# A planned order of instructions: modulation dot products move from GpSimd to VectorE, one chunk of them to the FFN, and the planner's durations change

## The chip, the cores and the metric

The kernel runs on one core of a Trainium2 chip. The metric is device time in microseconds from one launch, the median of several runs. The engines are named as in the profile: PE is TensorE, with PEld its weight loads; DVE is VectorE, ACT ScalarE, POOL GpSimd, SP the engine that issues most DMAs.

## The reference, cut to what matters

Two layers run over 512 latent tokens with a context of 256 tokens. Layer 0 mixes tokens by bidirectional gated linear attention (GLA, 4 heads), layer 1 by latent attention (MLA, 8 heads), and each is followed by a gated ConvFFN. Every sub-layer is modulated: six vectors of 1024 numbers per layer (shift, scale and gate of the mixer, then of the FFN) come from a condition, one condition for the latent tokens and one for the context.

```python
def ada_modulation(cond, w, b):
    m = jax.nn.silu(cond) @ w + b
    return jnp.split(m, 6, axis=-1)

def modulate(x, g, shift, scale):
    return rmsnorm(x, g) * (1 + scale[..., None, :]) + shift[..., None, :]

x = x + g1[:, None, :] * o
x = x + g2[:, None, :] * conv_ffn(modulate(x, norm_ffn[i], sh2, sc2), ...)
```

The six vectors are called chunks 0 to 5 here. Chunks 0 and 1 feed the first norm, 2 is the gate of the mixer (`g1`), 3 and 4 are shift and scale of the FFN's norm, and 5 is the gate of the FFN (`g2`), which is first needed where the FFN's first down product is added to the residual.

## The kernel before, in words

All activations are kept feature-major, [128 features, 768 tokens] per tile, and each weight tile of [128, 1024] is loaded into a ring of three staging buffers (`ws`), split exactly into a high part on ACT (`wh`) and a low part on DVE (`wl`), and used in three products on PE (`mm3`).

**The modulations.** A chunk has 8 tiles of 128 features. `ada` loads one tile of weights (`wa`, in the same ring of three as `ws`) and forms one dot product per condition against the condition's row `cb`. A dot on DVE is one instruction with an accumulated sum (`junk` in the rows), followed by a short read of the accumulator. The other way, in `ada_dot`, is a product on POOL (`wa<-wa,cb`, over the weights in place) and then a sum on ACT (`wa<-wa` with an accumulator); the staging buffer is free only after the ACT instruction. With two conditions, the first goes to DVE and the second to POOL and ACT. In layer 1, chunks 2 to 5 are needed for one condition only, and the two ways alternate (`flip`).

**Where they are made.** Chunks 0 and 1 of layer 0 are made in the start. In `gla`, each of the four heads is emitted by `weave`, which interleaves three streams: the products of this and the next head, the chain of the attention itself (`core`: transposes `ktp`, scores `scp` and `A`, states `stp` and `R`, outputs `ops` and `o`, transposed outputs `Got`), and one chunk of modulations (2, 4, 3, 5 in this order). In the FFN of layer 0, `extra(i)`, called behind the i-th pair of feature tiles, makes the modulations of layer 1, three tiles a time from i = 2.

**What sets the order.** `Later` records every instruction and `flush` puts them in the order of a list schedule: each engine takes the first recorded of those whose operands and buffers are ready, with durations from `cost` and delays from `after`. Only the order comes from there. On the chip, each engine executes its list in order and waits at the head of it, SP's DMA issues too. All instructions are issued from one line of `flush`, so that they share one line number (L263) in the profile.

Of the kernel before, what the change touches and what calls it, by code (L numbers as in the profile page):

```python
# [13 lines left out]
ALU = mybir.AluOpType  # L14
# [16 lines left out]
# columns of the vector table  # L31
# [14 lines left out]
# columns of the table of constants  # L46
# [6 lines left out]
# how the start is divided: feature tiles whose first modulations are products of the tensor engine, and  # L53
# (tile, shift or scale, condition) of those whose products GpSimd makes
# [5 lines left out]
MOD_STAGE = (0, 1, 2)  # tiles whose modulation weights come in the buffers of the other weights  # L60
# what arrives in turn: modulation weights of a feature tile, two tiles of the first weights, the context
START_LOADS = ("m0", "m1", "w0", "w1", "w2", "m3", "m2", "m5", "m4", "ctx", "w3", "m7", "m6")
COND_AFTER = (3, 7)  # tiles of squares after which the two conditions are taken
CTX_NORM = 5  # the step of the first products at which the norm of the context comes
CTX_LAG = 5  # steps of the context behind those of the latent tokens, not before its norm
NORM_POOL = (3, 6)  # the feature tiles of a latent norm that GpSimd and ScalarE modulate


def weave(*streams):
    """Emits the steps of several streams in proportion: (generator, its expected total, where it starts).  # L70
    A step is its time on the tensor engine, or its share of the total."""
    live = [[g, total, sum(start)] for g, total, *start in streams]
    while live:
        s = min(live, key=lambda x: x[2])
        try:
            step = next(s[0])
            s[2] += step[0] if isinstance(step, tuple) else step / s[1]
        except StopIteration:
            live.remove(s)


def paced(units):
    """Steps of units of work that count as equally long: (generator, its expected total)."""
# [18 lines left out]
class Later:  # L102
    """Records instructions and emits them when a pool ends, in the order of a list schedule.

    Every engine takes the first recorded of the instructions whose operands and buffers are ready; the costs are
    those of the guide. Only the order comes from here: Tile finds all waits anew, in the instructions so ordered."""
# [3 lines left out]
    def __init__(self, tc):  # L110
        self.tc, self.real = tc, tc.nc
        self.ops, self.preload = [], None
        self.seen = {}  # tile -> its accesses in this batch
        self.done = {}  # tile -> when its accesses end, from earlier batches
        self.held, self.tags = {}, {}  # tag, and tile of it -> (tag, the tiles in its buffers)
        self.old = {}  # tile -> the one before in its buffer
        self.free = dict.fromkeys(self.ENGINES, 0.6) | {"sync": 2.2}
        self.table = None
        # from the end of an instruction on one engine to the start of one that needs it on another
# [21 lines left out]
    def record(self, engine, op, args, kw):  # L141
        if op == "preload_act_table_set":
            # goes before the next activation, if that changes the table
# [5 lines left out]
        for x, write in aps:  # L149
            row = math.prod(x.tensor.shape[1:])  # L150
            lo = hi = x.offset % row
            # the elements of a partition: from lo to hi, and if they are few, which
# [19 lines left out]
        self.ops.append((engine, op, args, kw, preload, deps, {x.name for x, _ in aps}, *self.cost(engine, op, args, kw, aps)))  # L172

    @staticmethod
    def cost(engine, op, args, kw, aps):
        """time on the engine, and the activation table"""
# [4 lines left out]
        if engine == "tensor":  # L181
            if op == "transpose":
                return max(0.107, x.shape[-1] / 2400.0), None
            full = (args[1] if len(args) > 1 else kw["lhsT"]).dtype == F32
            return (max(0.213, n / 600.0) if full else max(0.107, n / 2400.0)), None
# [5 lines left out]
        n = max(math.prod(y.shape[1:]) for y, _ in aps)  # L191
        if engine == "vector":
# [3 lines left out]
        return (0.16 * n if kw.get("op") == ALU.pow else 0.1 + n / 450.0), None  # L196
# [1460 lines left out]
```

## Time and profile before

| what | value |
| --- | --- |
| median of 3 runs | 1679.93 us (1679.58 to 1681.09) |
| profiled execution, span from first to last instruction | 1679.1 us |
| PE busy in it | 1611.4 us (96%) |
| DVE busy | 1116.0 us (66%) |
| ACT busy | 720.4 us (43%) |
| POOL busy | 298.9 us (18%) |
| mean granted TensorE clock | 0.989 |

The profile gives no time of its own for the profiled execution beside its span; the median of the runs is 0.8 us above the span. The stages follow each other: the start (to about 80 us), the four GLA heads (80 to 385), the output product and the norm of the FFN (385 to 460), the FFN of layer 0 (460 to 1000), MLA (1000 to 1330) and the FFN of layer 1. A busy share near 100% on PE means that matmuls follow each other closely; PE's time at half clock counts as busy, so the granted clock (PEclk) has to be read beside it.

### The profile page before, as it was taken

What the parts mean: (1) busy time and instruction counts of PE and PEld (TensorE: products, weight loads), DVE (VectorE), ACT (ScalarE), POOL (GpSimd) and SP (SyncE); (2) the same over time, 40 slices, a digit from 0 to 9 for tenths busy, and PEclk for the clock granted to TensorE, in tenths of its full rate; (3) what the DMA queues carried; (4) which work ended last, traced back from release to release, by engine and by line L of the source; (5) the groups of instructions that cost most, each with busy time, mean ns of one, the idle gap of its engine ahead of it and who ended that gap; (6) DMA issues with size and microseconds to landing.
All of it is one profiled execution on the core that took longest, in us unless ns stands there. A gap on an engine that the chain in (4) does not pass through costs nothing.

```text
span 1679.1 us, 22918 instructions
## 1 busy us (share of the span) xinstructions
PE 1611.4 (96%) x9086; PEld 1386.0 (83%) x9086; DVE 1116.0 (66%) x1773; ACT 720.4 (43%) x1253; POOL 298.9 (18%) x170
## 2 busy tenths in 40 slices
PE   7899889889999999999999999999999999999999
PEld 4688778778888888888888888788889888888887
DVE  7977777885677855655544567777776765555554
ACT  4555444552443533323322336666653533333331
POOL 3223233330112411111100020334400100000000
PEclk9999999999999999999999999999999999999999
DMA  8222223233133343333331222100031232232232
GB/s 320 99 93 96 93 86 111 76 116 142 38 113 121 131 151 126 126 126 126 126 101 64 76 109 79 40 15 26 20 120 47 69 113 98 90 101 99 90 100 76
DMA packets 50079, 165.59 MB, mean 99 GB/s; under 512 B 5554, under 2 KB 7346, under 8 KB 49972
## 3 DMA queue, kind: packets, MB, share of 16 engines
q1 hardware_dynamic: 49332, 162.04, 28.2%
q0 software_dynamic: 640, 2.10, 0.3%
q8 instruction: 71, 1.16, 0.3%
q14 instruction: 36, 0.29, 0.1%
HBM read 159.92 MB, written 4.19 MB: 98 GB/s over the span
## 4 chain that ended last, share of the span: by engine, by line
PE 78%; DVE 10%; issue 5%; ACT 3%; DMA 2%; POOL 1%; SPq 0%; POOLq 0%; DVEq 0%; ACTq 0%
PE G L263 59%; PE Gs L263 4%; PE av L263 2%; PE ukv L263 2%; DVE K L263 2%; PE Gu L263 2%; DVE junk L263 2%; PE uq L263 1%; DMA wa<-in_wada 1%; PE pt L263 1%; DVE hl L263 1%; PE ops L263 1%; PE vps L263 1%; DVE R L263 1%; PE stp L263 1%
## 5 line engine op out<-in xcount | busy, mean ns | idle before, releaser
L263 PE MATMUL G<-hh,wh 128*128 128x512 f32 (+1 forms) x1416 | 507.0, 358 | 1.2 <-DVE x L263 1.2
L263 PE MATMUL G<-hl,wh 128*128 128x512 f32 (+2 forms) x1416 | 494.1, 350 | 0.2 <-DVE hl L263 0.2
L263 PE MATMUL G<-hh,wl 128*128 128x512 f32 (+1 forms) x1400 | 491.9, 351 | 0.0
L263 DVE TENSOR_TENSOR wl<-ws,wh 128x1024 fp32r<-128x1024 f32 (+3 forms) x178 | 222.4, 1251 | 270.2 <-ACT wh L263 268.7
L263 ACT CAST wh<-ws 128x1024 fp32r<-128x1024 f32 (+3 forms) x186 | 189.5, 1020 | 441.9 <-PE G L263 422.8
L263 PEld LDWEIGHTS G<-hh,wh 128*128 128x128 f32 x1416 | 267.4, 189 | 36.3 <-DVE x L263 1.4
L263 PEld LDWEIGHTS G<-hl,wh 128*128 128x128 f32 (+1 forms) x1416 | 266.7, 188 | 36.9 <-DVE hl L263 0.7
L263 PEld LDWEIGHTS G<-hh,wl 128*128 128x128 f32 x1400 | 264.3, 189 | 34.5
L263 POOL TENSOR_TENSOR wa<-wa,cb 128x1024 f32<-128x1024 f32 x64 | 168.4, 2634 | 524.3 <-DVE mod L263 263.2
L263 PE MATMUL G<-ph,wh 128*128 128x512 f32 (+1 forms) x512 | 181.8, 355 | 2.3 <-DVE z L263 2.3
L263 PE MATMUL G<-ph,wl 128*128 128x512 f32 (+1 forms) x512 | 182.1, 356 | 0.0
L263 PE MATMUL G<-pl,wh 128*128 128x512 f32 (+1 forms) x512 | 181.7, 355 | 0.0
L263 DVE SCALAR_TENSOR_TENSOR z<-G,vec,z 128x511 f32<-128x511 f32 x248 | 151.0, 651 | 1.7 <-ACT z L263 0.9
L263 DVE CUSTOM_DVE_ANT_0 junk<-wa,cb 128x1024 bf16<-128x1024 f32 x75 | 109.9, 1465 | 49.2 <-DMA wa<-in_wada 49.0
L263 PEld LDWEIGHTS G<-ph,wh 128*128 128x128 f32 x512 | 96.2, 188 | 16.9 <-issue 2.6
L263 PEld LDWEIGHTS G<-pl,wh 128*128 128x128 f32 x512 | 96.1, 188 | 14.8
L263 PEld LDWEIGHTS G<-ph,wl 128*128 128x128 f32 x512 | 96.1, 188 | 13.9
L263 ACT ACTIVATE wa<-wa 128x1024 f32<-128x1024 f32 x64 | 67.6, 1057 | 66.4 <-POOL wa L263 66.3
L263 DVE SCALAR_TENSOR_TENSOR x<-G,mod,x 128x512 f32<-128x512 f32 (+1 forms) x112 | 64.8, 610 | 35.2 <-PE G L263 34.7
L263 ACT ACTIVATE z<-G,vec 128x768 f32<-128x768 f32 (+1 forms) x82 | 72.4, 883 | 3.1 <-PE G L263 2.3
L263 ACT ACTIVATE z<-z 128x768 f32<-128x768 f32 (+1 forms) x44 | 32.5, 739 | 93.2 <-DVE z L263 93.2
L263 DVE SCALAR_TENSOR_TENSOR y<-G,mod,y 128x512 f32<-128x512 f32 (+1 forms) x72 | 49.2, 688 | 21.3 <-PE G L263 20.7
(343 smaller groups left out, 2673.0 us busy)
## 6 DMA issues: line engine op xcount, KB each, us to landing
wa<-in_wada SPq DMA_DIRECT2D x90, 512.0 KB, 3.5
ws<-in_wup SPq DMA_DIRECT2D x88, 512.0 KB, 3.3
ws<-in_wdn SPq DMA_DIRECT2D x44, 512.0 KB, 3.5
ws<-in_win SPq DMA_DIRECT2D x13, 512.0 KB, 3.3
ws<-in_wmd SPq DMA_DIRECT2D x9, 512.0 KB, 3.3
ws<-in_wv SPq DMA_DIRECT2D x8, 512.0 KB, 3.7
ws<-in_wog SPq DMA_DIRECT2D x8, 512.0 KB, 3.6
ws<-in_womh SPq DMA_DIRECT2D x8, 512.0 KB, 5.6
```

Of the source, the lines that this page charges most:

```text
L263: getattr(getattr(self.real, engine), op)(*args, **kw)
```

## The change

1. `ada_chunk`, which makes the chunks of layer 0 after the start, calls `ada` with `alone=True`: both dots of a tile are DVE instructions, without POOL and ACT. The modulations of layer 1 stay as they were.
2. Chunk 5 leaves the GLA heads. Chunks 2, 4 and 3 are spread over the four heads (6, 7, 6 and 5 tiles, where there were 8 in each). Chunk 5 is made by `extra(0)` and `extra(1)`, four tiles each, in the FFN of layer 0.
3. `cost` has other durations for transposes, products, scans and powers, and a new function `shares` marks instructions of DVE and POOL that, in the plan, can't run beside each other: the plan starts one after the other's end.

```diff
+        self.port = {"vector": 0.0, "gpsimd": 0.0}
...
             if op == "transpose":
-                return max(0.107, x.shape[-1] / 2400.0), None
+                return 0.109, None
-            return (max(0.213, n / 600.0) if full else max(0.107, n / 2400.0)), None
+            return (max(0.22, n / 590.0) if full else max(0.109, 0.0063 + n / 2296.0)), None
...
+        if op == "tensor_tensor_scan":
+            return 0.07 + n / 480.0, None
...
-        return (0.16 * n if kw.get("op") == ALU.pow else 0.1 + n / 450.0), None
+        return (0.9 + 0.17 * n if kw.get("op") == ALU.pow else 0.1 + n / 450.0), None
+
+    @staticmethod
+    def shares(engine, op, aps):
+        reads = [x for x, write in aps if not write and x.space != PSUM and math.prod(x.shape[1:]) > 1]
+        if engine == "gpsimd":
+            return bool(reads) and op != "dma_start"
+        fast = op in ("tensor_scalar", "tensor_copy") and aps[0][0].space != PSUM
+        return engine == "vector" and (len(reads) > 1 or bool(reads) and fast)
...
-            cost, table = ops[i][7:]
+            cost, table, shares = ops[i][7:]
+            if shares:
+                t = max(t, self.port[e])
...
             self.free[e] = end[i] = t + cost
+            if shares:
+                self.port["gpsimd" if e == "vector" else "vector"] = t + cost
...
-    def ada(self, layer, chunk, nt, conds):
+    def ada(self, layer, chunk, nt, conds, alone=False):
         wa = self.ada_load(layer, chunk, nt)
         self.flip ^= len(conds) == 1
         for c in conds:
-            self.ada_dot(wa, layer, chunk, nt, c, None if self.flip or len(conds) == 2 and c == 0 else wa)
+            self.ada_dot(wa, layer, chunk, nt, c, None if alone or self.flip or (len(conds) == 2 and c == 0) else wa)
...
-    def ada_chunk(self, layer, ch, conds=(0, 1)):
-        for nt in range(8):
-            self.ada(layer, ch, nt, conds)
+    def ada_chunk(self, layer, ch, conds=(0, 1), nts=range(8)):
+        for nt in nts:
+            self.ada(layer, ch, nt, conds, True)
             yield 1.0
+        if nts[-1] < 7:
+            return
         self.ada_bias(layer, ch, conds)
...
-                (self.ada_chunk(0, 2), 8.0),
+                (self.ada_chunk(0, 2, nts=range(6)), 6.0),
...
-                (self.ada_chunk(0, 4), 8.0),
+                (seq(self.ada_chunk(0, 2, nts=range(6, 8)), self.ada_chunk(0, 4, nts=range(5))), 7.0),
...
-                (self.ada_chunk(0, 3), 8.0),
+                (seq(self.ada_chunk(0, 4, nts=range(5, 8)), self.ada_chunk(0, 3, nts=range(3))), 6.0),
...
-                (self.ada_chunk(0, 5), 8.0),
+                (self.ada_chunk(0, 3, nts=range(3, 8)), 5.0),
...
             def extra(i):
+                if i < 2:
+                    run_all(self.ada_chunk(0, 5, nts=range(4 * i, 4 * i + 4)))
```

What the plan makes of it is seen in the engines' lists. First POOL from the end of the start through the four heads, before: `wa` are the products of modulations, `orr` the inverse root of the output norm of a head, `nr` that of a norm of tokens, `ny` a norm's product.

```order
L263 TENSOR_TENSOR wa<-wa,cb 128x1024 x6
L263 TENSOR_TENSOR orr<-orr,mhalf 128x6
L263 TENSOR_TENSOR wa<-wa,cb 128x1024 x8
...
L263 TENSOR_TENSOR wa<-wa,cb 128x1024 x2
L263 TENSOR_TENSOR nr<-nr,mhalf 128x4
```

And now, up to the FFN of layer 0:

```order
L280 TENSOR_TENSOR prod<-wa_117,cb 128x1024
L280 TENSOR_TENSOR nr<-nr,mhalf 128x2
L280 TENSOR_TENSOR orr<-orr,mhalf 128x6 x4
L280 TENSOR_TENSOR nr<-nr,mhalf 128x4
L280 TENSOR_TENSOR ny<-x_3197,nrb 128x512
L280 TENSOR_TENSOR ny<-x_3200,nrb 128x512
L280 TENSOR_TENSOR nr<-nr,mhalf 128x2
L280 TENSOR_TENSOR wa<-wa,cb 128x1024 x32
```

The 32 products between the start and the output product are gone; the four `orr` stand alone, and the 32 products for layer 1 remain behind the norm of the FFN.

Second, DVE in the first head, in the forward states (`R` with its factor `cf` carries the state from one block to the next, `A` are masked scores, `junk` is a dot, `ISA mod` its accumulator). Before:

```order
L263 TENSOR_TENSOR R_703<-stp,R_700 128x256
L263 TENSOR_TENSOR A<-scp,kon 128x128
L263 TENSOR_SCALAR R_703<-R_703,cf_663 128x256
L263 COPY_PREDICATED A<-kon,scp 128x128
L263 TENSOR_TENSOR R_706<-stp,R_703 128x256
L263 ISA junk,mod_68<-wa,cb 128x1024
L263 ISA mod_68 128x1
L263 TENSOR_SCALAR R_706<-R_706,cf_663 128x256
```

Now:

```order
L280 TENSOR_TENSOR R_703<-stp,R_700 128x256
L280 ISA junk,mod_68<-wa,cb 128x1024
L280 ISA mod_68 128x1
L280 TENSOR_SCALAR R_703<-R_703,cf_663 128x256
L280 TENSOR_TENSOR A<-scp,kon 128x128
L280 TENSOR_TENSOR R_706<-stp,R_703 128x256
L280 COPY_PREDICATED A<-kon,scp 128x128
L280 TENSOR_SCALAR R_706<-R_706,cf_663 128x256
L280 TENSOR_TENSOR A<-scp,kon 128x128
L280 ISA junk,mod_68<-wa,cb 128x1024
L280 ISA mod_68 128x1
L280 COPY_PREDICATED A<-kon,scp 128x128
```

A dot now stands between the two halves of an earlier step of the recurrence, and more of them follow in the later steps.

Third, DVE in the norm before the FFN of layer 0, where `x` is the residual of the context, `nacc` its sum of squares, `ny` and `hl` the normed latent tokens that the FFN's first products wait for. Before:

```order
L263 TENSOR_TENSOR nacc<-nacc,nsq 128x256
L263 SCALAR_TENSOR_TENSOR x_3266<-G,mod_68,x_3266 128x256
L263 SCALAR_TENSOR_TENSOR hl<-ny,mod_68,hh 128x512 x2
L263 SCALAR_TENSOR_TENSOR ny<-x_3262,gain_3289,nrb 128x512
L263 SCALAR_TENSOR_TENSOR x_3267<-G,mod_68,x_3267 128x256
```

Now:

```order
L280 SCALAR_TENSOR_TENSOR x_3199<-G,mod_68,x_3199 128x256
L280 ISA junk,mod_68<-wa,cb 128x1024
L280 ISA mod_68 128x1
L280 TENSOR_TENSOR nacc<-nacc,nsq 128x256
L280 ISA junk,mod_68<-wa,cb 128x1024
L280 ISA mod_68 128x1
L280 SCALAR_TENSOR_TENSOR x_3200<-G,mod_68,x_3200 128x256
L280 ISA junk,mod_68<-wa,cb 128x1024
L280 ISA mod_68 128x1
L280 SCALAR_TENSOR_TENSOR hl<-ny,mod_68,hh 128x512 x2
L280 ISA junk,mod_68<-wa,cb 128x1024
L280 ISA mod_68 128x1
```

Four of the sixteen dots of chunk 5 now stand around the first `hl`; the other twelve stand among the first three pairs of the FFN.

## Rows read from the trace of the kernel before

**Rows 1.** The page: span, and the group of POOL's modulation products.

```profile
span 1679.1 us, 22918 instructions
...
L263 POOL TENSOR_TENSOR wa<-wa,cb 128x1024 f32<-128x1024 f32 x64 | 168.4, 2634 | 524.3 <-DVE mod L263 263.2
```

**Rows 2.** Stretches: start to end, length, then busy us of each engine, PEclk, DMA.

```profile
0.00:80.00 80.00, 60.53 (x302) 42.81 (x303) 66.77 (x113) 39.45 (x69) 27.58 (x15) 0.98 0.58 212
80.00:385.00 305.00, 274.13 (x1701) 246.50 (x1700) 235.99 (x348) 151.37 (x266) 93.92 (x36) 0.96 0.30 104
...
430.00:460.00 30.00, 29.73 (x208) 27.31 (x207) 23.21 (x43) 15.28 (x27) 4.59 (x3) 1.00 0.14 52
460.00:560.00 100.00, 97.65 (x561) 85.39 (x560) 75.25 (x106) 41.47 (x53) 23.94 (x10) 1.00 0.32 111
560.00:1000.00 440.00, 440.00 (x2545) 387.60 (x2544) 252.94 (x365) 145.76 (x178) 64.50 (x33) 1.00 0.34 116
1000.00:1330.00 330.00, 321.45 (x2041) 276.88 (x2040) 243.26 (x530) 192.68 (x493) 82.48 (x74) 0.99 0.16 51
```

**Rows 3.** PE's waits in the GLA heads (80 to 385): us, times, longest.

```profile
PE ops L263 <- DVE R L263: 8.0, 5, 2.9
PE Got L263 <- DVE o L263: 7.1, 4, 2.0
PE vps L263 <- ACT v L263: 5.8, 2, 3.1
PE ktp L263 <- DVE K L263: 5.7, 2, 4.5
PE stp L263 <- ACT KT L263: 3.4, 1, 3.4
```

**Rows 4.** DVE in order of time in the second head: start, us, instruction.

```profile
163.70 1.21 DVE L263 CUSTOM_DVE_ANT_0 junk<-wa,cb 128x1024 bf16<-128x1024 f32 x1
164.84 0.07 DVE L263 DVE_READ_ACCUMULATOR2_ANT mod<- 128x1 f32 x1
...
165.71 3.14 DVE L263 TENSOR_TENSOR K<-K,k 128x768 f32<-128x768 f32 x1
...
170.96 0.96 DVE L263 TENSOR_TENSOR K<-K,md 128x768 f32<-128x768 f32 x1
...
173.85 3.11 DVE L263 TENSOR_TENSOR K<-K,k 128x768 f32<-128x768 f32 x1
```

**Rows 5.** POOL in order of time, beside rows 4.

```profile
165.05 2.99 POOL L263 TENSOR_TENSOR wa<-wa,cb 128x1024 f32<-128x1024 f32 x1 [2.17 <-ACT v L263]
```

**Rows 6.** DVE in the first head, a scaling of the state.

```profile
112.27 0.34 DVE L263 TENSOR_SCALAR R<-R,cf 128x256 f32<-128x256 f32 x1
```

**Rows 7.** DVE's groups by shape, 80 to 385: busy us, mean ns, idle before.

```profile
L263 DVE CUSTOM_DVE_ANT_0 junk<-wa,cb 128x1024 bf16<-128x1024 f32 x32 | 47.6, 1487 | 9.8 <-DMA wa<-in_wada 9.7
...
L263 DVE TENSOR_SCALAR R<-R,cf 128x256 f32<-128x256 f32 x32 | 24.7, 771 | 0.6
L263 DVE TENSOR_TENSOR K<-K,k 128x768 f32<-128x768 f32 x8 | 15.6, 1959 | 0.6 <-ACT K L263 0.6
L263 DVE TENSOR_SCALAR o<-o,orr 128x256 f32<-128x256 f32 x24 | 15.1, 693 | 3.6 <-POOL orr L263 3.6
...
L263 DVE TENSOR_TENSOR Q<-Q,t 128x768 f32<-128x768 f32 x8 | 12.1, 1514 | 4.6 <-ACT t L263 4.6
```

**Rows 8.** ACT's groups, 80 to 385: the sum behind POOL's product.

```profile
L263 ACT ACTIVATE wa<-wa 128x1024 f32<-128x1024 f32 x32 | 33.9, 1059 | 37.9 <-POOL wa L263 37.8
```

**Rows 9.** SP's queue, 80 to 385: whom its DMA issues waited for.

```profile
SPq L263 <- ACT wa L263: 160.3, 23, 14.6
```

**Rows 10.** The chain that ended last, 80 to 385, shares by engine and tile.

```profile
by line: issue 22.5%; PE G L263 18.2%; DVE K L263 8.7%; DMA wa<-in_wada 7.8%; DVE junk L263 6.0%; PE ops L263 5.6%; PE vps L263 4.8%; DVE R L263 4.2%; PE stp L263 4.2%; DVE o L263 2.9%; PE scp L263 2.8%; DVE Q L263 2.7%; ACT t L263 2.5%; AC
```

**Rows 11.** The second GLA head as a stretch; columns as in rows 2.

```profile
160.00:235.00 75.00, 64.73 (x384) 57.65 (x384) 52.53 (x75) 30.96 (x57) 22.50 (x9) 0.93 0.27 92
```

**Rows 12.** PE's waits from 385 to 560.

```profile
PE G L263 <- DVE z L263: 2.3, 2, 1.5
```

More of the change, by code (lines that the diff above doesn't have):

```diff
@@ L171, in record @@
             preload, self.preload = self.preload, None
-        self.ops.append((engine, op, args, kw, preload, deps, {x.name for x, _ in aps}, *self.cost(engine, op, args, kw, aps)))
+        self.ops.append((engine, op, args, kw, preload, deps, {x.name for x, _ in aps}, *self.cost(engine, op, args, kw, aps), self.shares(engine, op, aps)))
     @staticmethod
@@ L446, in ada @@
         for c in conds:
-            self.ada_dot(wa, layer, chunk, nt, c, None if self.flip or len(conds) == 2 and c == 0 else wa)
+            self.ada_dot(wa, layer, chunk, nt, c, None if alone or self.flip or len(conds) == 2 and c == 0 else wa)
     def ada_bias(self, layer, chunk, conds):
```

## The prediction

> **What bounds the kernel now.** The page gives a span of 1679.1 us and 64 modulation products on POOL [rows 1]. I read the stretches next [rows 2]. In the FFN of layer 0, from 560 to 1000 us, PE is busy for all of 440.00 us at full clock: nothing on another engine can shorten it. In the four GLA heads (80 to 385) PE is busy for 274.13 of 305 us at a granted clock of 0.96. This is the stage that the change works on, so the next view is who makes PE wait there. The five largest waits [rows 3] sum to 8.0 + 7.1 + 5.8 + 5.7 + 3.4 = 30.0 us, and 20.8 of these end with a DVE instruction: a state `R`, a scaled output `o`, a decayed key `K`. The clock adds 305 x (1 - 0.96) = 12.2 us, as far as PE was at work meanwhile. So about 42 us, and no more, can be won in the heads.
>
> Then I ask why DVE is late. It is busy for 235.99 of 305 us [rows 2], but not all of this is work. Two instructions of one form and size, both with two inputs in SBUF, took 0.96 and 3.14 us [rows 4], and the long one ran beside a POOL product of 2.99 us that had begun at 165.05 [rows 5]: it ended as that one did, plus its own time. The second `K<-K,k`, at 173.85, took 3.11. By the Trainium skill, page "SBUF — State Buffer", section "SBUF: two separate sides", the port pair of DVE and GpSimd is an exclusive lock, held for a whole instruction; these rows agree. By that rule alone each of the 32 products could hold one DVE instruction for up to its whole length of 2.63 us, 84 us in all; I use the rows of the DVE groups instead.
>
> **The port's price.** Five groups of DVE in the heads [rows 7] against their undisturbed durations [rows 4, 6]: dots 32 x (1.487 - 1.21) = 8.9 us; states 32 x (0.771 - 0.34) = 13.8; `K<-K,k` 8 x (1.959 - 0.96) = 8.0; outputs, of the states' form and size, 24 x (0.693 - 0.34) = 8.5; `Q<-Q,t`, of the keys' form, 8 x (1.514 - 0.96) = 4.4. Together 43.6 us of DVE's 236.0 are waiting for POOL.
>
> **What the change removes in the heads.** All 32 POOL products there go; what POOL keeps is one inverse root per head. With them go 32 sums on ACT, 33.9 us [rows 8], which stood in ACT's queue ahead of copies that PE waits for. The staging buffers also come free earlier: SP's queue waited 160.3 us in 23 waits for just those sums [rows 9], the landing of modulation weights is 7.8% of the chain, 24 us [rows 10], and DVE stood idle for 9.7 us until such a load had landed [rows 7]. I give the DMA part no term of its own, as DVE must still wait for a load where it stands in front; it is a reason for the gain not to be at its lower end.
>
> **What it adds in the heads.** 24 tiles with two dots each make 48, where there were 32 on DVE: 16 more, at 1.21 + 0.07 us [rows 4], 20.5 us. DVE goes from 236.0 to 236.0 - 43.6 + 20.5 = 212.9 us: less, with more instructions. But the dots stand in the middle of the recurrence: behind such a dot wait a state, the scores behind it, and PE's `ops`. Per head the dots number 12, 14, 12 and 10, before 8 each.
>
> **What is left of PE's waits.** I go through [rows 3] one by one. `Got <- o`, 7.1 us, comes from the first `o` waiting for a product that POOL started just behind the inverse root; nothing of that kind is left: 1 us remains. `ktp <- K`, 5.7: the two `K` lose 2.2 us each, and the ones queued behind come earlier: 1 remains. `stp <- KT`, 3.4, hangs on the same keys: 1 remains. `vps <- ACT v`, 5.8: ACT's copy stands behind exponentials that wait for DVE's `K` and behind the sums: 3 remain. `ops <- R`, 8.0: the states lose the port but get more dots ahead of them: 5 remain. That is 11 of 30.0, so 19 us go. The 12.2 us of the clock go with the waits, as far as one sees: the second head, where PE waited longest at a time, 4.5 us, has the lowest clock, 0.93 [rows 11], against 0.96 for all four. I take that 7 of the 12.2 go. **Heads: -26 us.** The bounds are -42 (all waits and all of the clock) and +8 (the rival below).
>
> **The FFN of layer 0.** Sixteen dots of chunk 5 arrive, 16 x 1.28 = 20.5 us on DVE, between the norm and the third pair. DVE was busy for 23.21 of 30 us from 430 to 460 and for 75.25 of 100 from 460 to 560 [rows 2], so 31.5 us are idle there and the dots fit, at 92%, if they are spread evenly. They are not quite: four stand around the first `hl`, which the first up products wait for, and dots go ahead of splits and convolutions of the next tiles. PE's largest wait here was 2.3 us, on the convolution [rows 12]. Against that, POOL's products for layer 1 start later, and their place is the long stretch after 560, where DVE is busy for 253 of 440 us [rows 2]. The last DVE work that these feed is due only at the end of the FFN, so that they cost nothing; if this cover were gone, it would be at most the 20.5 us by which they are pushed back. The ends are 0 and +20.5; I take **+3 us**, near the lower, since the idle time exceeds the dots.
>
> **The new order elsewhere.** The durations in the plan also reorder the start and MLA. In the start the tiles now come in their natural order, and PE has products for the modulations of tile 2 ahead of the first products of tile 0; the inverse root of the context's norm is behind three POOL products. PE idles for 19.5 of 80 us there [rows 2], mostly for first loads. In MLA PE idles for 8.6 of 330. I know of no instruction there that is shorter. Both get 0, with -5 to +5 for the start and -4 to +4 for MLA.
>
> **Sum:** span 1679.1 - 26 + 3 = 1656.1 us; the median of the runs was 0.8 above the span, so **1657 us**.
>
> **The rivals.**
> *Slower: dots in front of the recurrence.* On the chain the dots hold 6.0% of 305 us, 18.3 [rows 10], for 32 dots. In the new list 48 dots take 48 x 1.28 = 61.4 us. If DVE's queue became the path itself, with nearly every dot ahead of a state or a key that PE waits for, the path would gain up to 43.1. The heads and the FFN give -23, so it breaks even when 18.3 + 23 = 41.3 of the 61.4 us, two thirds of the dots, lie on the path; at 80% it is 49.1 - 41.3 = +8, 1688 us. For it speaks the new list of DVE in the first head, with a dot inside most steps. Against it: PE has products of the next head to do meanwhile, and only 18.3 of the 47.6 us of dots [rows 7], 38%, were on the chain even with the port's waits in them. The Trainium skill, page "Perfetto Trace Analysis", section "Optimizing Scalar/DVE Operations", is on this rival's side where it says that work may be offloaded from a saturated DVE even to GPSIMD; it adds that the shared port may make that useless, and the rows above agree with the addition.
> *No change: other waits take their place.* `R` waits for `stp`, and that for `R`: if the recurrence alone set the heads' length, freeing DVE would only move the idle time. Then 1677 to 1683. Against it: the waits that go are at keys and outputs, outside the recurrence.
> *The FFN takes back more.* If the dots around the first `hl` and among the first pairs delay PE by half of their time, +10, and the heads give only 20: 1670.
> *The heads give all.* Waits of 3 us and hardly a drop of the clock: -38, FFN +1: 1643.
>
> **How the numbers follow.** A measurement of this kernel can tell about 0.2%, 3.4 us, from no change. My forecast (gain 14 to 30 us) has 0.60, the FFN's rival 0.17, the heads giving all 0.09, no change 0.05, slower 0.09. The range takes in the first three as far as the bounds allow: 42.2 us less is 1638 at the low end; half of the heads' gain (13) with 8 lost in the FFN is 1674 at the high end. Faster 0.86, same 0.05, slower 0.09.
>
> **What would show it.** In the changed profile: no POOL product between 80 us and the output product; `K<-K,k` at 0.96, states at 0.34 and dots at 1.21 us on average in the heads; PE's waits there near 11 us and PEclk near 0.98; `ops <- R` the largest of what is left; up to a few us of PE waits on `hl`, `wl` or `z` around the FFN's start. I am wrong if DVE's groups become short and the heads don't, or if the FFN's first 100 us grow by 10.

## The result and the profile after

The change makes the kernel 1.2% faster: 1659.67 us (median of 4 runs, 1658.88 to 1660.02) against 1680.14 us in the same session, a ratio of 0.9878 with a 95% interval of 0.9864 to 0.9892. The forecast was 1657.0 us, with a range of 1638 to 1674. The total came out nearly as worked out, and the parts did not, as the stages show. The profiled execution of after took 1660.02 us, 1.7 above its span. Its page, the span and POOL's group, which answer to [rows 1]:

```profile
span 1658.3 us, 22865 instructions
...
L280 POOL TENSOR_TENSOR wa<-wa,cb 128x1024 f32<-128x1024 f32 x32 | 83.6, 2619 | 331.5 <-DMA wa<-in_wada 147.6
```

A stage begins here where PE's order of time shows its first product: the heads with the first `Gz` (the first gate product), the output product and norm behind the last `Got`, the FFN of layer 0 with its first `Gu` (up products), MLA with its first `Gc` (its first projections), and the rest with the first `Gu` of the second FFN. These marks fit both kernels, which the fixed stretches of [rows 2] do not. The heads and the FFN between the marks, before (columns as in [rows 2]):

```profile
80.95:377.07 296.12, 265.25 (x1640) 238.34 (x1639) 227.30 (x338) 148.67 (x262) 90.92 (x35) 0.95 0.28 96
...
443.32:999.32 556.00, 553.38 (x3195) 486.41 (x3193) 342.41 (x498) 197.01 (x248) 92.28 (x45) 1.00 0.33 112
```

After, from the start to MLA:

```profile
0.00:88.93 88.93, 64.69 (x311) 46.31 (x311) 63.90 (x114) 41.09 (x70) 26.45 (x15) 0.90 0.53 192
88.93:343.46 254.53, 253.08 (x1660) 230.60 (x1659) 193.77 (x376) 116.49 (x201) 5.87 (x4) 1.00 0.33 109
343.46:405.81 62.35, 61.11 (x362) 54.07 (x361) 33.02 (x51) 18.29 (x27) 1.01 (x1) 1.00 0.23 76
405.81:973.57 567.76, 556.38 (x3194) 488.14 (x3193) 366.65 (x527) 196.78 (x248) 94.23 (x44) 0.99 0.36 116
973.57:1285.71 312.14, 302.94 (x1882) 258.32 (x1881) 225.53 (x501) 183.00 (x472) 78.34 (x70) 0.99 0.16 50
```

Before, the start was 80.95 us long, the norm's stretch 66.25 and MLA 307.02. Read by length: start +8.0, heads -41.6, output product and norm -3.9, FFN +11.8, MLA +5.1, the rest -0.1, in sum -20.7 of a span that went from 1679.1 to 1658.3 us. A gain of 45 us is there; 25 of it are given back in three other stages. Each length is read from one profiled execution.

**The heads.** PE is busy for 253.08 of 254.53 us at a granted clock of 1.00. Its idle time fell by 29.4 us and its busy time, which holds what the clock costs, by 12.2; together they are the 41.6. Two waits are left, 1.5 us where [rows 3] had 30.0 (PE's waits in the heads of after):

```profile
PE vps L280 <- ACT v L280: 1.0, 2, 0.5
PE ops L280 <- DVE R L280: 0.5, 1, 0.5
```

DVE's groups there stand at the durations that [rows 4, 6] had for an undisturbed one (after, DVE in the heads; to be laid beside [rows 7]):

```profile
L280 DVE CUSTOM_DVE_ANT_0 junk<-wa,cb 128x1024 bf16<-128x1024 f32 x48 | 58.5, 1218 | 6.6 <-DMA wa<-in_wada 6.3
...
L280 DVE TENSOR_SCALAR R<-R,cf 128x256 f32<-128x256 f32 x32 | 11.1, 348 | 0.5
...
L280 DVE TENSOR_TENSOR Q<-Q,t 128x768 f32<-128x768 f32 x8 | 7.7, 956 | 7.2 <-ACT t L280 7.2
L280 DVE TENSOR_TENSOR K<-K,k 128x768 f32<-128x768 f32 x8 | 7.6, 955 | 0.0
```

The mean of `K<-K,k` went from 1959 to 955 ns, that of `R<-R,cf` from 771 to 348. DVE does 16 more dots and is busy for 33.5 us less. The 32 sums of [rows 8] are gone from ACT, and with them the 160.3 us that SP's queue waited for them [rows 9]; its largest wait is now for the splits (SP's waits in the heads, after):

```profile
SPq L280 <- DVE wl L280: 107.2, 19, 18.3
```

**The FFN.** One wait of PE is long, 8.4 us (PE's waits in the FFN of layer 0, after):

```profile
PE G L280 <- DVE x L280: 8.4, 1, 8.4
...
PE G L280 <- DVE z L280: 1.1, 2, 0.7
```

DVE in order of time ahead of that `x`, the residual sum of the first down products (after; columns as in [rows 4]):

```profile
464.46 1.23 DVE L280 CUSTOM_DVE_ANT_0 junk<-wa,cb 128x1024 bf16<-128x1024 f32 x1 [0.21 <-DMA wa<-in_wada]
...
466.48 3.37 DVE L280 CUSTOM_DVE_ANT_0 junk<-wa,cb 128x1024 bf16<-128x1024 f32 x1
...
469.78 0.95 DVE L280 TENSOR_TENSOR pl<-z,ph 128x768 fp32r<-128x768 f32 x1
470.65 3.35 DVE L280 CUSTOM_DVE_ANT_0 junk<-wa,cb 128x1024 bf16<-128x1024 f32 x1
...
473.94 1.80 DVE L280 SCALAR_TENSOR_TENSOR x<-G,mod,x 128x512 f32<-128x512 f32 x3
```

And POOL beside it:

```profile
465.77 3.00 POOL L280 TENSOR_TENSOR wa<-wa,cb 128x1024 f32<-128x1024 f32 x1 [49.74 <-DVE mod L280]
469.99 2.94 POOL L280 TENSOR_TENSOR wa<-wa,cb 128x1024 f32<-128x1024 f32 x1 [1.22 <-ACT wa L280]
```

These are the first dots of layer 1, which still use POOL. They reach DVE just ahead of `x`, and two of the three run beside a POOL product and take 3.37 and 3.35 us where one alone took 1.23: the lock that left the heads stands here instead. Before, the same three dots began at 475.64, 484.47 and 493.15 us, some 9 us apart and none of them beside a product, and `x` followed at 500.05. An estimate from these rows: two dots longer by 2.1 us each make some 4.3 of the 8.4 us, and the rest is that the three stand in one bunch in front of `x`. PE's last product before the wait began at 466.45, the next one at 475.12, and the clock went with it, as two stretches show (after; columns as in [rows 2]):

```profile
466.00:476.00 10.00, 1.61 (x9) 1.30 (x8) 10.00 (x10) 4.07 (x6) 7.55 (x3) 0.79 0.26 64
476.00:490.00 14.00, 14.00 (x71) 12.03 (x71) 9.41 (x13) 6.03 (x8) 5.35 (x3) 0.91 0.53 181
```

**The start.** PE's largest wait there was 4.0 us for `hh` before; now it is 10.9, 6.8 of them at one time (PE's waits in the start, after):

```profile
PE Gq L280 <- ACT hh L280: 10.9, 4, 6.8
...
PE adp L280 <- DMA wa<-in_wadk: 3.4, 2, 2.8
```

The 6.8 us can be followed back through ACT and POOL in order of time (after, 36 to 55 us; `prod` is a POOL product of the start):

```profile
52.60 1.06 ACT L280 ACTIVATE prod<-prod 128x1024 f32<-128x1024 f32 x1 [7.80 <-POOL prod L280]
...
53.65 0.71 ACT L280 ACTIVATE hh<-x,mod 128x512 fp32r<-128x512 f32 x1
```

```profile
36.87 3.38 POOL L280 TENSOR_TENSOR prod<-wa,cb 128x1024 f32<-128x1024 f32 x1 [1.26 <-ACT prod L280]
50.22 2.34 POOL L280 TENSOR_TENSOR prod<-wa,cb 128x1024 f32<-128x1024 f32 x1 [9.97 <-DMA wa<-in_wada]
```

POOL stood idle for 9.97 us until a load of modulation weights had landed; its product, ACT's sum and `hh` follow one another, and PE's next `Gq` begins at 54.41. That load is the last of its batch in SP's list, behind two of `ws` and two of `x`:

```profile
39.75 0.33 SPq L280 DMA_DIRECT2D wa<-in_wada  x1
```

The clock went here too: 0.90 over the start, where it was 0.98 before and 0.94 in the run e10 below, which has the old start. Of the 8.0 us PE was idle for 4.8 more and busy for 3.2 more (64.69 us, before 61.48).

### The profile page after: what moved, and what is told of

The parts are those of the page before. It is cut to its first block, busy times and chain, and to the rows that moved or that the text cites. A ratio compares the mean times of both kernels' runs of the same rounds, so it can differ in the third digit from the quotient of the medians.

```text
span 1658.3 us, 22865 instructions
## 1 busy us (share of the span) xinstructions
PE 1604.3 (97%) x9086; PEld 1381.7 (83%) x9086; DVE 1095.4 (66%) x1837; ACT 687.0 (41%) x1189; POOL 209.2 (13%) x138
## 4 chain that ended last, share of the span: by engine, by line
PE 69%; DVE 4%; ACT 1%; DMA 1%; issue 0%; POOL 0%
PE G L280 54%; PE Gs L280 5%; PE av L280 2%; PE Gu L280 2%; PE ukv L280 2%; PE uq L280 2%; PE pt L280 1%; DVE junk L280 1%; DVE z L280 1%; DMA wa<-in_wada 1%; DVE wl L280 0%; DVE hl L280 0%; PE kt L280 0%; PE qpt L280 0%; DVE ny L280 0%
## 5 line engine op out<-in xcount | busy, mean ns | idle before, releaser
L280 DVE TENSOR_TENSOR wl<-ws,wh 128x1024 fp32r<-128x1024 f32 (+3 forms) x178 | 217.1, 1221 | 254.9 <-ACT wh L280 252.8
L280 DVE CUSTOM_DVE_ANT_0 junk<-wa,cb 128x1024 bf16<-128x1024 f32 x107 | 142.3, 1330 | 48.4 <-DMA wa<-in_wada 47.8
L280 POOL TENSOR_TENSOR wa<-wa,cb 128x1024 f32<-128x1024 f32 x32 | 83.6, 2619 | 331.5 <-DMA wa<-in_wada 147.6
L280 PE MATMUL vps<-wh,hh 128*128 128x256 f32 x192 | 53.9, 281 | 1.0 <-ACT v L280 1.0
```

Source lines behind the costliest of these rows:

```text
L280: getattr(getattr(self.real, engine), op)(*args, **kw)
```

## The experiments

Twelve kernels were run. The changed kernel has three parts: no POOL products in the heads (dots), chunk 5 in the FFN, and the new plan, which itself is two things, other durations and the rule of the shared port (`shares`). The stage lengths of all, by the marks above, are worked out from the first and last PE instructions of each stage; the time is the median of the runs, for `e3` one run. Ratios are to the kernel before in the same session, whose median lay between 1678.81 and 1681.07 us.

```
                     start  heads  norm   FFN 0   MLA   rest   time us   ratio to before, 95%
before                81.0  296.1  66.2   556.0  307.0  372.7  1680.14
after                 88.9  254.5  62.4   567.8  312.1  372.5  1659.67   0.9878 [0.9864, 0.9892]
e1_plan_alone         88.7  263.7  60.8   556.3  311.2  373.1  1656.68   0.9866 [0.9834, 0.9897]
e2_dots_alone         81.6  250.1  65.7   564.5  306.9  373.8  1646.32   0.9805 [0.9779, 0.9832]
e3_no_product         83.4  250.7  65.7   556.3  306.7  371.7  1636.24   one run
e4_start_before       82.4  254.8  62.3   567.1  309.9  372.5  1652.30   0.9844 [0.9817, 0.9872]
e5_port_rule          83.0  267.5  60.5   556.8  311.0  375.8  1656.71   0.9863 [0.9834, 0.9893]
e6_durations          82.5  288.6  64.3   556.8  307.2  371.3  1672.76   0.9974 [0.9955, 0.9992]
e7_dots_later         80.9  251.3  66.1   558.5  306.7  371.2  1638.36   0.9768 [0.9733, 0.9803]
e8_after_later        87.6  254.9  62.3   557.5  311.1  371.0  1646.70   0.9802 [0.9769, 0.9835]
e9_middle_new         81.1  249.9  64.8   557.4  307.0  371.3  1635.43   0.9734 [0.9714, 0.9754]
e10_all_in_heads      81.6  251.4  65.1   556.3  305.7  372.7  1635.12   0.9736 [0.9717, 0.9755]
e11_best              83.6  251.7  64.3   555.7  307.0  374.0  1636.11   0.9737 [0.9713, 0.9760]
e12_idle_products     82.3  275.8  65.1   556.3  307.1  371.4  1660.39   0.9874 [0.9846, 0.9903]
```

The starts with the old plan took 80.9 to 83.6 us, so that 2 or 3 us more or less there say nothing.

My theory was that the heads gain because POOL's products no longer hold DVE's port. The rivals: that the new plan makes the gain, or that ACT's sums and the staging buffers do.

### The parts alone

**e1_plan_alone**: the kernel before with the new `cost` and `shares`; the modulations as they were (the diff is against after, cut).

```diff
-                (self.ada_chunk(0, 2, nts=range(6)), 6.0),
+                (self.ada_chunk(0, 2), 8.0),
...
-            self.ada(layer, ch, nt, conds, True)
+            self.ada(layer, ch, nt, conds)
...
-                if i < 2:
-                    run_all(self.ada_chunk(0, 5, nts=range(4 * i, 4 * i + 4)))
```

> The kernel before with the planner's new durations and its port rule alone; the modulations are made where and how they were, 8 tiles per head, half of the dots as products on GpSimd. If the heads' gain (296.1 us from the first gate product to the last transposed output before, 254.5 after) comes from the dots that left GpSimd, the heads stay at 280 to 296 us here, and the start (81 us before, 89 after) and MLA (307 before, 312 after) take the changed kernel's lengths: 1675 to 1693 us in all. If the planner's better durations made the gain, the heads fall to 255 to 265 and the time to 1645 to 1660.

The heads took 263.7 us and the kernel 1656.68, so the theory missed and the other branch came true: the plan alone takes 32 us from the heads, while all 32 products stay on POOL. **e2_dots_alone** is the other half, the changed kernel with the old plan; `cost_before` is the `cost` of the kernel before (against after, cut).

```diff
+        self.old_plan = True
...
-        self.ops.append((engine, op, args, kw, preload, deps, {x.name for x, _ in aps}, *self.cost(engine, op, args, kw, aps), self.shares(engine, op, aps)))
+        self.ops.append((engine, op, args, kw, preload, deps, {x.name for x, _ in aps}, *(self.cost_before if self.old_plan else self.cost)(engine, op, args, kw, aps), not self.old_plan and self.shares(engine, op, aps)))
```

> The changed kernel with the old durations and no port rule in the planner: the dots and chunk 5 as changed. If the dots made the heads' gain, the heads take 255 to 270 us; start and MLA have the order of before, 81 and 307 us; the FFN of layer 0 keeps its stall: 1645 to 1660 us. If the gain needs the planner's durations, the heads take 280 us or more: 1670 to 1690.

The heads took 250.1 us, 46 less than before and 5 below the range expected, and the kernel is some 13 us faster than the whole change. Each part shortens the heads, but they do not add: with the dots in place, the new plan has nothing left to gain there and makes them 4 us longer (250.1 to 254.5). Start and MLA are at their old lengths (81.6, 306.9), so what after loses there, 8 and 5 us, is the plan's; the FFN's stall is there without the plan (564.5, with a wait of 6.8 us for `x`).

**e4_start_before** gives the start of after its old plan and changes nothing else (cut; `old_plan` as in e2, but off at first).

```diff
+        nc.old_plan = True
         H, (Gq, Gk, mr, mu) = self.start(st)
         stp.close()
+        nc.old_plan = False
```

> The changed kernel with the planner's old durations up to the end of the start, the new ones after it. If the start's 8 us more come from the plan alone, PE reaches the first gate product at 81 us instead of 89 and the time is 1650 to 1653. Rival (the heads would have waited for loads anyway): under 3 us of it come back, 1657 to 1660.

The start took 82.4 us, as with the old plan elsewhere, and the time fell to 1652.30 (7.4 us by the medians, some 6 by the ratios), so the start's loss is the plan's in the start itself, and the heads don't take it back.

### Which half of the plan

**e5_port_rule** has the rule of the port with the old durations, **e6_durations** the new durations without the rule; both with the modulations of before. The diffs are against e1.

```diff
-        self.ops.append((engine, op, args, kw, preload, deps, {x.name for x, _ in aps}, *self.cost(engine, op, args, kw, aps), self.shares(engine, op, aps)))
+        self.ops.append((engine, op, args, kw, preload, deps, {x.name for x, _ in aps}, *self.cost_before(engine, op, args, kw, aps), self.shares(engine, op, aps)))
```

> The kernel before with the rule of the shared port alone in the list schedule: its old durations, its dots and its 32 products on GpSimd stand. With durations and rule together the same dots gave 1656.7 us, with heads of 263.7, a start of 88.7 and a first attention of 311.2. Theory (an order that knows of the port puts work that has time behind the products, so the rule alone hides the waits): heads 260 to 270, start near 81 and attention near 307, a time of 1640 to 1655. Rival (the old durations were too short, PE's work was put too close behind VectorE's, and the new durations give the slack): heads 285 to 297 and a time of 1668 to 1681. Which of the two also lengthens the start by 8 us is told by the same run: 88 to 89 if the rule does it, 81 to 82 if the durations do.

```diff
-        self.ops.append((engine, op, args, kw, preload, deps, {x.name for x, _ in aps}, *self.cost(engine, op, args, kw, aps), self.shares(engine, op, aps)))
+        self.ops.append((engine, op, args, kw, preload, deps, {x.name for x, _ in aps}, *self.cost(engine, op, args, kw, aps), False))
```

> The kernel before with the new durations alone in the list schedule, no rule of the port, its dots and its 32 products on GpSimd as they were. Theory (the rule hides the waits): heads as before, 285 to 297, a start of 81 to 89, a time of 1668 to 1690. Rival (the durations give the slack): heads 260 to 270, a time of 1645 to 1660. If the start is near 88 here and near 81 with the rule alone, the durations cost the 8 us there.

The rule takes 28.6 us from the heads, the durations 7.5; in both the heads came as the theory had them. In e5 POOL's products take as long as before. Its heads as a stretch, and PE's four largest waits there:

```profile
83.02:350.52 267.50, 260.43 (x1690) 234.82 (x1688) 222.28 (x345) 150.48 (x265) 91.07 (x36) 1.00 0.34 115
```

```profile
PE Got L305 <- DVE o L305: 2.7, 2, 1.9
PE stp L305 <- DVE R L305: 1.8, 2, 1.4
PE stp L305 <- DVE A L305: 1.2, 2, 0.9
PE vps L305 <- ACT v L305: 0.6, 1, 0.6
```

and DVE's groups and POOL's products there:

```profile
L305 DVE CUSTOM_DVE_ANT_0 junk<-wa,cb 128x1024 bf16<-128x1024 f32 x32 | 47.0, 1470 | 9.5 <-DMA wa<-in_wada 9.5
L305 DVE TENSOR_TENSOR wl<-ws,wh 128x1024 fp32r<-128x1024 f32 x24 | 35.4, 1486 | 4.9 <-ACT wh L305 4.8
L305 DVE TENSOR_SCALAR R<-R,cf 128x256 f32<-128x256 f32 x32 | 19.9, 621 | 0.4
```

```profile
L305 POOL TENSOR_TENSOR wa<-wa,cb 128x1024 f32<-128x1024 f32 x32 | 85.8, 2683 | 181.6 <-DVE mod L305 111.9 <-ACT t L305 28.9 <-ACT o L305 16.1
```

DVE is busy for 222.28 us in these heads, hardly less than the 227.30 of before: its instructions still wait for the port. Yet PE's waits fall from 30.7 us, all of them counted, to 7.1, and the clock is 1.00. In e5 the `wl` of a later tile waits more (1486 ns against 1220 undisturbed) and the states less (621 against 771). But in e1 the states wait longer than before (926 ns) and the heads are shorter still (263.7 us), so the means of the groups do not tell whose delay PE feels. That the rule puts work with time to spare behind the products is the likely reading; no run shows it instruction by instruction. The Trainium skill, page "SBUF — State Buffer", section "Summary: rules for kernel authors", advises to schedule whichever of the two engines is off the critical path. The plan's rule does not look at that path, but e5 is on the side of the advice: an order alone made the heads 28.6 us shorter.

Neither half alone lengthens the start beyond what other runs with the old plan show (83.0 and 82.5); only both together do (88.7 in e1, 88.9 in after), which neither expectation had. In e1, POOL waits 9.13 us in the start for the same kind of load and PE 5.9 us behind it, as in after. So the late load comes from the one order that the two make together. MLA's 4 us come with the rule (311.0), not with the durations (307.2); with them the time of e5, 1656.71, lies just above its range. Why the rule is worse there was not tried; after has `Gkr` waiting 1.7 us for DVE's `vl`, and 2.4 in place of 0.9 us on `ukv`.

### The port, or what hangs on the products

**e3_no_product** is the kernel before without the 32 products; ACT's 32 sums stay.

```diff
-    def ada_dot(self, wa, layer, chunk, nt, c, prod=None):
+    def ada_dot(self, wa, layer, chunk, nt, c, prod=None, bare=False):
...
-            nc.gpsimd.tensor_tensor(prod, wa, self.cb[:, c], op=ALU.mult)
+            if not bare:
+                nc.gpsimd.tensor_tensor(prod, wa, self.cb[:, c], op=ALU.mult)
             nc.scalar.activation(prod, prod, AF.Identity, accum_out=col)
...
-            self.ada_dot(wa, layer, chunk, nt, c, None if self.flip or len(conds) == 2 and c == 0 else wa)
+            self.ada_dot(wa, layer, chunk, nt, c, None if self.flip or len(conds) == 2 and c == 0 else wa, layer == 0)
```

> The kernel before without the 32 GpSimd products of chunks 2 to 5 of layer 0: ScalarE sums the raw weights in their place, so the context's modulations of these chunks are other numbers. VectorE's dots, ScalarE's sums and the staging buffers' chain stay, 2.6 us shorter for want of the product; only GpSimd's hold on the port goes. Port theory: VectorE loses its 43.6 us of waiting, keys take 0.96 us each, the heads 255 to 272 us, 1640 to 1660 in all. Rival (ScalarE's sums in front of copies, and the staging buffers they hold, made the heads long): the heads stay at 285 to 296 us, 1670 to 1680.

The heads took 250.7 us and the one run 1636.24, both below their ranges, with one wait of PE, 0.2 us, and ACT's sums all there (the heads as a stretch, and the sums):

```profile
83.35:334.00 250.65, 250.26 (x1641) 227.76 (x1640) 175.42 (x342) 147.79 (x264) 5.87 (x4) 1.00 0.39 125
...
L263 ACT ACTIVATE wa<-wa 128x1024 f32<-128x1024 f32 x32 | 33.9, 1060 | 16.4 <-DVE mod L263 16.1
```

So ACT's work for the sums costs the heads nothing. But the run leaves two things open. Without the products, ACT's sums and the staging buffers no longer wait for POOL either (33.3 us of ACT's waits in the heads of before). And the plan puts the engines' lists in another order when the products are gone. **e12_idle_products** puts 32 products back that nobody waits for (against e3, cut); PE's and DVE's lists stay nearly those of e3.

```diff
             if not bare:
                 nc.gpsimd.tensor_tensor(prod, wa, self.cb[:, c], op=ALU.mult)
+            else:
+                first = self.mod[layer][:, 0, chunk * 8 + nt : chunk * 8 + nt + 1].broadcast_to([P, D])
+                nc.gpsimd.tensor_tensor(self.idle, self.cb[:, 0], first, op=ALU.mult)
             nc.scalar.activation(prod, prod, AF.Identity, accum_out=col)
```

> The kernel of e3_no_product (the kernel before, its 32 products on GpSimd in the heads left out, ScalarE summing the raw weights instead, so that half of the modulations in chunks 2 to 5 of layer 0 are not the reference's; 1636.2 us, heads 250.7), with 32 products put back on GpSimd that nobody waits for: the condition's row times a column of the first dot, from SBUF into a tile of their own. ScalarE, the staging buffers and the loads wait for none of them; only GpSimd's queue (the inverse root `orr`) and VectorE's port see them. Theory (the shared port is what made the heads long): VectorE's groups are long again, and the heads take 275 to 296, the time 1660 to 1680. Rival (the heads were long because ScalarE's sums, and the copies behind them, waited for GpSimd's products): 251 to 262 and 1636 to 1648. In between, both: the share of the 45 us is read from the heads.

The heads took 275.8 us, 25.1 more than in e3, of the 45.4 that separate e3 from before. PE's waits are back, though no data hang on the products (the heads of e12 as a stretch, and PE's waits there):

```profile
82.29:358.07 275.78, 256.52 (x1643) 231.02 (x1642) 215.58 (x342) 148.60 (x264) 79.94 (x36) 0.99 0.35 114
...
PE vps L263 <- ACT v L263: 8.3, 4, 2.8
PE ktp L263 <- DVE K L263: 6.3, 3, 2.8
PE ops L263 <- DVE R L263: 2.8, 3, 1.5
```

and DVE's groups are long again, beside POOL's:

```profile
L263 DVE CUSTOM_DVE_ANT_0 junk<-wa,cb 128x1024 bf16<-128x1024 f32 x32 | 46.4, 1451 | 1.4 <-DMA wa<-in_wada 1.1
...
L263 DVE TENSOR_SCALAR R<-R,cf 128x256 f32<-128x256 f32 x32 | 25.6, 800 | 0.7
```

```profile
L263 POOL TENSOR_TENSOR idle<-cb,mod 128x1024 f32<-128x1024 f32 x32 | 73.8, 2305 | 194.7 <-DVE mod L263 172.2 <-DVE cf L263 22.3
```

DVE is busy for 215.58 us against 175.42 in e3, so these products hold it for 40.2 us. The port, with POOL's queue in front of `orr`, thus makes 25 of the 45 us. The other 20 lie between ACT's wait for the products, the staging buffers, the order of the lists, which is another in the kernel before, and the products themselves (2305 ns in the mean here); this was not taken apart further. The heads came at the lower end of the theory's range.

### The FFN's stall, and the best kernel

**e7_dots_later** (on e2) and **e8_after_later** (on after) begin the dots of layer 1 two pairs later.

```diff
-                for ch, nt in jobs[max(i - 2, 0) * 3 : max(i - 1, 0) * 3]:
+                for ch, nt in jobs[max(i - 4, 0) * 3 : max(i - 3, 0) * 3]:
...
-                if i == 18:
+                if i == 20:
```

> The changed kernel with the old list schedule (durations and no port rule), which took 1646.3 us, and the dots of layer 1 in the first FFN two pairs later, so that they begin behind the first down products. Theory (the residual sums of the first down products stand on VectorE behind three dots that wait for GpSimd's products, a stall of PE of 8 us there): the stall goes, the first FFN takes 556 to 559 in place of 564.5, and the time is 1637 to 1641. Rival (the eight dots of chunk 5 in the first two pairs lengthen the FFN by themselves, or the stall moves two pairs on, to the next down products): the first FFN stays at 562 to 566 and the time at 1643 to 1648.

> The changed kernel as it is, with the dots of layer 1 in the first FFN two pairs later and nothing else. Theory (the stall of 8.4 us at 467 is the FFN's loss): the first FFN takes 557 to 561 in place of 567.8 and the time falls from 1659.7 to 1649 to 1653; start and heads stay at 88.9 and 254.5. Rival (the stall moves on with the dots): 565 to 568 and no change of the time.

The FFN took 558.5 us in e7 and 557.5 in e8, as the theories had it, and the times fell by 8.0 and 13.0 us, which put e8 below its range. In e8 no wait for `x` is left. So of the 11.8 us that the FFN lost, 10.3 were this one stall with the clock behind it, and not the sixteen dots as work.

**e10_all_in_heads** keeps from the change only that POOL's products are gone: the old plan, and chunk 5 back in the fourth head (against e2, cut; the other three heads have their 8 tiles again too).

```diff
-                (self.ada_chunk(0, 3, nts=range(3, 8)), 5.0),
+                (self.ada_chunk(0, 5), 8.0),
...
-                if i < 2:
-                    run_all(self.ada_chunk(0, 5, nts=range(4 * i, 4 * i + 4)))
```

> The changed kernel with the old list schedule (1646.3 us) and chunk 5 back in the fourth head: 64 dots on VectorE in the heads, none of them in the FFN, the dots of layer 1 where they were. It makes of the change only that GpSimd's products are gone. Theory (VectorE has room in the heads once no product holds it, and what chunk 5 does in the FFN is to push the layer 1 dots in front of the first down products): heads 250 to 256, the first FFN 556 to 558, 1638 to 1645. Rival (64 dots are too many for VectorE in the heads, the waits come back): heads 258 to 270 and 1648 to 1660.

Heads 251.4, FFN 556.3, 1635.12 us, some 24 less than the whole change and 3 below the range expected. In the program the dots of layer 1 stand where e2 has them, whose FFN took 564.5, so the stall needs chunk 5 in front of them. The heads of e10 hold 64 dots as well as 48 (DVE 206.30 of 251.36 us):

```profile
81.64:333.00 251.36, 251.11 (x1643) 228.70 (x1642) 206.30 (x403) 114.97 (x200) 5.87 (x4) 1.00 0.39 123
```

From there to the end of the FFN PE waits for three things (e10):

```profile
PE G L305 <- DVE z L305: 2.2, 2, 1.4
PE G L305 <- DVE x L305: 1.3, 1, 1.3
PE rows L305 <- POOL nr L305: 1.0, 2, 0.7
```

**e9_middle_new** and **e11_best** add the new plan from the output product to the end of the FFN, to e7 and e10 (cut).

```diff
+            nc.old_plan = False
             with tc.tile_pool(name="wog", bufs=1, reuse_waits="tile") as wp:
...
             adas.close()
+            nc.old_plan = True
```

> The kernel of e7_dots_later (dots of layer 1 two pairs later, old list schedule, 1638.4 us) with the new schedule (durations and rule) from the output products of the linear attention to the end of the first FFN, and the old one in the start, the heads, the attention and the rest. From the stages of the runs so far: the norm before the FFN took 66.1 us with the old schedule and 62.3 with the new, the rest is to stay. Theory (the schedule's effect belongs to the stage that it plans): 1634 to 1637. Rival (the 4 us are only handed on, as PE waits for the FFN's first weights instead): 1637 to 1641.

> The kernel of e10_all_in_heads with the new schedule from the output products of the linear attention to the end of the first FFN. If both theories hold (all 64 dots fit in the heads, the new schedule shortens the norm by 4 us), 1633 to 1640; if the heads are too full, 1644 to 1656.

The norm came to 64.8 and 64.3 us, a gain of about 1 and not of 4, and the times, 1635.43 and 1636.11, cannot be told from e10's 1635.12. Both times lie in their ranges, but not by the 4 us that they were expected from. The norm's 4 us in after are thus not the plan's in that stage alone. The three are equally good; e10 is the simplest.

## Why the prediction was right, and where its steps were not

**The total was right by luck: errors of both signs cancelled.** Forecast -26 in the heads, +3 in the FFN, 0 in the start and in MLA: -23. Measured -41.6, +11.8, +8.0, +5.1, and -3.9 in the norm, for which I had no term: -20.7 with the 0.1 of the rest. So the terms were off by -15.6, +8.8, +8.0, +5.1 and -3.9 us, and their sum by 2.3. What lies around the span was 1.7 us, where I had taken 0.8.

**What bounds, and the port as DVE's delay: right.** e12 shows that products which nobody waits for lengthen the heads by 25 us. The five groups that I priced came to 43.6 us of DVE; e12's 32 products held it for 40.2 us. In the heads of before DVE carried more than the five groups: 227.30 - 175.42 = 51.9 us went in e3, since the splits `wl` (1378 ns before, 1220 after) and small instructions such as the factors `cf` waited too.

**Heads -26, the step "That is 11 of 30.0, so 19 us go": mis-sized.** I went through PE's waits one by one and let a piece of each stand; 1.5 us stood, `vps` the largest and not `ops`. The clock went from 0.95 to 1.00, all of it and not 7 of 12.2. After the change DVE's groups are as long as undisturbed ones and DVE has a quarter of its time free (193.77 of 254.53 us busy), and nothing of the waits that I priced remained. That free time alone does not ensure this is what the FFN shows. The measured -41.6 is my outer bound of -42. The other bound, +8, was no bound of the heads: it is the slower rival's change of the whole time, with the FFN's +3 in it.

**The dots in the recurrence (the slower rival): wrong, and by far.** 48 dots on DVE left PE waiting 0.5 us for `R`, and with e10's 64 dots the view of PE's waits in the heads is empty.

**No change by other waits: wrong**, the recurrence did not hold PE once the port was free. **The heads give all: right in the heads** (-38 forecast, -41.6).

**FFN +3, the step "near the lower, since the idle time exceeds the dots": wrong.** Idle time is a sum, and the stall was one place. I looked for the delay around `hl` and priced what POOL's later products cost at nothing because their results are due late. What they delayed was something else: the queue behind them, `x`, which frees the accumulators that PE needs. The profile of before had the price (3.14 us for 0.96) but I did not apply it to the FFN, where the 32 products remain. The rival that the FFN takes back +10 had the right size, and another place. My own sign of being wrong, the FFN's first 100 us longer by 10, came true: from 490 us on, 84 us into the FFN, PE is busy for 482.87 of 483.57 us at a clock of 1.00, so nearly all of the 11.8 us were lost ahead of that.

**Start 0 and MLA 0: wrong.** The start's +8.0 lies beyond its bound of 5; MLA's +5.1 lies just beyond its bound of 4, and around it in e8 and e4, which have the new plan there too (311.1 and 309.9 us against 307.0). I had named two orders in the start (PE's products for tile 2, and the inverse root behind three products). Only the first shows, as a wait of 2.8 us for `wadk`; PE's wait of 3.8 us for an inverse root, which before had, is gone. The larger wait of 6.8 us hangs on a load that comes late in SP's queue, through POOL and ACT. I costed a new list by what I saw move on PE and POOL, and not by the loads.

**"I give the DMA part no term":** DVE's idle time ahead of a dot for the load of `wa` went from 9.7 to 6.3 us; nothing against it.

## What to carry to other kernels

Price an offload to GpSimd by the VectorE instructions that it holds and by who waits behind those, not by its own busy time; where the products must stay, an order made with the port in mind gives back much of it (28.6 of 45 us here). A list schedule that knows more of the engines is not better in every stage: here it won in the heads and lost in the start and in MLA, so look at each stage by itself, and keep the old order where the new one loses. Moved work is to be followed to the place in the queue where it lands: free time on the engine, 31.5 us of it by my sum, did not prevent a stall of 8 us in front of one instruction.

## What the runs showed of the hardware that I had not expected

Instructions that move almost nothing wait for the port as well. The factors `cf`, one element per partition, in the heads (DVE's groups by shape), first of after, where POOL is nearly idle, then of e12 with its idle products:

```profile
L280 DVE TENSOR_TENSOR cf<-cf,K 128x1 f32<-128x1 f32 x8 | 0.9, 156 | 0.0
```

```profile
L263 DVE TENSOR_TENSOR cf<-cf,K 128x1 f32<-128x1 f32 x8 | 6.0, 788 | 0.0
```

So an instruction's size does not tell what the lock can cost it: eight of these small ones lost 5.1 us together. The plan's rule takes no account of them, as `shares` counts only reads of more than one element per partition. The dot with an accumulator is held like the others, 3.37 us for 1.23. And e5 shows how little the lock need cost the path in another order: PE waited some 7 us with 85.8 us of products beside it.
